# Heads 12 and 13 of a dilated attention layer: queries and keys moved through DRAM instead of transposed on TensorE

## The chip, the cores and the metric

One core of one Trainium2 chip runs the whole kernel. The metric is the device time of one execution in microseconds (us). Beside it stands a profile of one execution, whose span runs from its first to its last instruction. In the text TensorE (PE in the profile) multiplies matrices, VectorE is DVE, ScalarE is ACT, GpSimd is POOL, and SyncE (SP) issues nearly all DMAs; its queue runs in order.

## The reference

An encoder block of two layers on 512 tokens of width 1024, 16 heads of 64. Only the first layer is touched here. In it every head has three dilation groups (dilations 1, 4, 16), each with its own queries, keys and values, and the three results are merged by their softmax denominators:

```python
def mixer_a(hn, w_in, w_out, q_gain, k_gain, t5_bias):
    proj = hn @ w_in
    qkv = proj[..., :n_qkv].reshape(b, s, N_DIL_GROUPS, 3, N_HEADS, HEAD_DIM)
    gate = proj[..., n_qkv:]
    for g, (window, dilation) in enumerate(DILATED_PAIRS):      # (128, 1), (512, 4), (2048, 16)
        q = rms_norm(qkv[:, :, g, 0], q_gain[g])
        k = rms_norm(qkv[:, :, g, 1], k_gain[g])
        v = qkv[:, :, g, 2]
        o, lse = dilated_group_attention(q, k, v, t5_bias[...], dilation, reach)
        ...
    alpha = jax.nn.softmax(jnp.stack(lses), axis=0)
    y = jnp.sum(alpha[..., None] * jnp.stack(outs), axis=0)
    y = y.reshape(b, s, BRANCH_WIDTH) * jax.nn.silu(gate)
    return y @ w_out
```

The second layer (neighbourhood attention) follows on the sum of input and output, with the same kind of projections, gate and output product.

## The kernel before

Heads go in pairs: hc = 0 to 7 counts pairs, NHC = 8, and heads 12 and 13 are hc = 6. For each pair main_a issues four projections, each a run of matmuls with 512 columns: the keys of groups 1 and 2 with their values (rawk, 96 matmuls), the queries of all three groups with the keys of group 0 (rawq, 96), the values of group 0 (v0_a, 24) and the gate (gate_a, 24). Products are taken in three matmuls each (high and low parts of both operands), so three matmuls are the smallest group. For hc = 7 rawq stands ahead of rawk, and gate 6 comes after both: rawq(7), rawk(7), gate(6), v0(7), gate(7). Then follows the output projection, out_product.

A projection is gathered in four PSUM banks (ps_acc), one for each quarter of the tokens; a bank is free again when ScalarE has evicted it (line 551). After the last quarter the rows are normalised for each head (head_norm): squares on GpSimd (line 317), a sum on VectorE, the factor rs by rsqrt on VectorE or GpSimd, and a scaling on VectorE (line 337).

Scores want queries and keys with the head dimension on the partitions. There are two ways to it.

- For hc = 0 to 5 (moved(hc)): VectorE turns blocks of 32 by 32 in place (turn_raw, line 588), move_q writes the tile rq of queries and keys to a DRAM tile qd (1.5 MB), and four reads bring it back into qt in the other order (lines 722 and 729). Then split_q on ScalarE scales and copies into k0 and three areas of queries (lines 793 and 777).
- For hc = 6 and 7: k_a and q_a transpose on TensorE, four blocks of 128 by 128 at a time (transpose4), two times for k_a and four for q_a, and evict each four with one instruction into qt and k0 (lines 679, 705, 712, 793).

The values of group 0 already take a similar way through DRAM (move_v) for hc = 0 to 6.

attn_a computes the scores of a pair in two halves, u = 0 and u = 1, 96 matmuls in the profile each ("log"). Each half goes through softmax on VectorE and ScalarE (p), is turned on VectorE into tr, written to DRAM (td) and read back into pt (class turner). When both halves are back, weigh() multiplies with the values ("o") and put_y applies the gate. weigh of pair hc is run inside the first half of pair hc + 1 ("pending").

The order on TensorE is the order of the program. Two generators make it: main yields after each group of three projection matmuls, and run() lets side insert its pieces when they are due. Due times are counted on a clock that adds an estimate for each matmul:

```python
        cols = max(r.free_size() / 2.4, l.free_size() / 1.2)
        clock[0] += (cols if r.dtype == F32R else r.free_size() * 4 / 2.4 * l.free_size() / P) / share
```

`yield "wait", (key, hc), 6500` makes the side wait until the stamp (key, hc) is set and the clock has gone 6500 beyond it; `later_on(delay, job)` puts a job, mostly a DMA, into the program at clock + delay. A guard, such as ("q", hc - 1) in main_a, keeps the last step of a projection from being issued before the stamp is set. The tiles rq (raw queries and keys), qt, k0, tr and pq are single buffers. The other engines' orders come from the scheduler, apart from instructions pinned by keep_in_program_order. Weights are loaded by SyncE in pieces of 512 KB (wraw, three buffers), split by splits() into high and low parts (wh and wl, four buffers each) on ScalarE, VectorE and GpSimd, at least three pieces ahead of use.

Of the kernel before, what the change touches and what calls it, by code (L numbers as in the profile page):

```python
# [26 lines left out]
NHC = 8  # L27
# [25 lines left out]
def tile_hybrid_encoder(  # L53
# [168 lines left out]
                yield h[:, c : c + n], l[:, c : c + n]  # L222

    clock = [0.0]
    stamp = {(key, -1): 0 for key in ("k12", "q", "v", "qk")}
    stamp |= {(key, -i, "y"): 0 for key in ("ya", "yb") for i in range(1, 6)}

    def matmul(o, l, r, share=1, **kw):
# [283 lines left out]
        fs, f0, f1 = FS[key]  # L512
        return rq[:, : 512 * fs].rearrange("p (a x) -> p a x", a=4)[:, :, P * f0 : P * f1]

    moved = lambda hc: hc < NHC - 2

    def part(n):
        return rk[:, 1024 * n : 1024 * n + 1024].rearrange("p (i c) -> p i c", i=4)
# [57 lines left out]
        normed(raw, ss, ns, key, hc)  # L576

    def normed(raw, ss, ns, key, hc):
        delay = (11000 if moved(hc) else 9000) if key == "rawk" and 0 < hc < NHC - 1 else 0
        head_norm(raw, ss, ns, delay, then=partial(turn_raw, key) if moved(hc) else None)  # L580
        st[key, hc] = raw
        stamp[key, hc] = clock[0]

# [49 lines left out]
    def move_v(hc, vt):  # L633

        d = dr.tile([4, P, P], F32, name="vd", tag="vd", bufs=2)
        vx = vv[:, S:].rearrange("p (b i r) -> p b i r", b=4, i=4)
        nc.vector.transpose(vx.rearrange("p b i r -> p i b r"), vt.rearrange("p (i b r) -> p i b r", i=4, b=4))

        def write():
            tc.keep_in_program_order(nc.sync.dma_start(d.rearrange("b p x -> p b x"), vx.rearrange("p b i r -> p b (i r)")))  # L640

        def read(b):
            dst = vt[32 * b : 32 * b + 32].rearrange("k (a x) -> k a x", a=4)
            tc.keep_in_program_order(nc.sync.dma_start(dst, d[b].rearrange("(a k) x -> k a x", a=4)))

        def place():
            src = vt.rearrange("p (a i r) -> p i a r", a=4, i=4)
            dst = v0[hc % 2].rearrange("p i (a r) -> p i a r", a=4)
            tc.keep_in_program_order(nc.scalar.copy(dst, src))
            stamp["v", hc] = 0  # L650

        out, back, there = (8000, 15000, 23500) if moved(hc) else (8000, 13000, 18500)
        later_on(out, write)
        for b in (0, 2, 1, 3):
            later_on(back, partial(read, b))
        later_on(there, place)

    def main_a(hc):
        parts = (
            project_qk(512, 4, "rawk", hc, ("k12" if hc == NHC - 1 else "q", hc - 1), first=hc == 0, need=None if hc else "na"),  # L660
            project_qk(512, 8, "rawq", hc, ("q", hc - 1) if hc else ("rs", "a")),
        )
        yield from chain(*(parts[::-1] if hc == NHC - 1 else parts))
        if hc == NHC - 1:
            yield from gate_a(hc - 1)
        yield from v0_a(hc)
        if hc != NHC - 2:
            yield from gate_a(hc)

    def k_a(hc):  # L670
        if moved(hc):
            return
        yield "wait", ("rawk", hc), 35000 if hc < NHC - 1 else 10500
        qt = q_tiles(hc)[0]
        raw = st.pop(("rawk", hc))
        for g in range(2):
            tp = transpose4(raw, g * P)
            dst = qt[:, :, 4 + g, :].rearrange("p t (j r) -> p t j r", j=4)
            nc.vector.tensor_scalar(dst, to_tjr(tp), gk[:, g + 1 : g + 2], None, op0=ALU.mult)
            yield  # L680
        stamp["k12", hc] = 0

    def q_tiles(hc):

# [7 lines left out]

    def q_a(hc):

        yield "wait", ("rawq", hc), 8000 if moved(hc) else 18500 if hc < NHC - 1 else 23500
        raw = st.pop(("rawq", hc))
        if moved(hc):
            move_q(hc)
            return
        qt, k0 = q_tiles(hc)  # L700

        by_t = lambda to: qt[:, :, to, :].rearrange("p t (x r) -> p x t r", x=16)
        of_t = lambda tp: tp.rearrange("p (x t r) -> p x t r", x=16, t=4)
        tp = transpose4(raw, 0)
        nc.scalar.copy(by_t(0), of_t(tp))
        yield
        tp = transpose4(raw, 3 * P)
        scaled(trj(k0[:, 64:EXT]), to_trj(tp), 0)
        yield
        for g in range(2):  # L710
            tp = transpose4(raw, (g + 1) * P)
            nc.vector.tensor_copy(by_t(1 + g), of_t(tp))
            yield
        stamp["q", hc] = 0

    def move_q(hc):

        d = dr.tile([4, P, 768], F32, name="qd", tag="qd", bufs=2)
        left = [4]

        def write():
            tc.keep_in_program_order(nc.sync.dma_start(d.rearrange("a p x -> p a x"), rq.rearrange("p (a x) -> p a x", a=4)))
            stamp["q", hc] = 0

        def read(a):
            qt, _ = q_tiles(hc)
            dst = qt[32 * a : 32 * a + 32].rearrange("k t f x -> k t (f x)")
            src = d[a].rearrange("(t k) x -> k t x", t=4)
            tc.keep_in_program_order(nc.sync.dma_start(dst, src))
            left[0] -= 1  # L730

        later_on(600, write)

        def land():
            for a in (0, 2, 1, 3):
                later_on(6500, partial(read, a))
            yield "wait", ("rawk", hc + 1), 0
            assert not left[0]
            split_q(hc, *q_tiles(hc))
            yield  # L740

        st["land", hc] = land
# [35 lines left out]

    def v_a(hc):

        if hc < NHC - 1:
            return
        yield "wait", ("vt", hc), 2500
        vt = st.pop(("vt", hc))
        tp = bank("tp")
        for i in range(4):
            transpose(tp[:, i * P : (i + 1) * P], vt[:, i * P : (i + 1) * P])
        nc.scalar.copy(v0[hc % 2], tp.rearrange("p (i c) -> p i c", i=4))
        stamp["v", hc] = 0
        yield  # L790
# [148 lines left out]
    def attn_a(hc):  # L939
# [114 lines left out]

        if hc < NHC - 1:
            for u in range(2):
                if moved(hc):
                    if u == 0:
                        yield "wait", ("rawk", hc + 1), 6500
                    elif hc < NHC - 3:  # L1060
                        yield "wait", ("open", hc + 1), 2500
                    else:
                        yield "wait", ("rawq", hc + 1), 2500
                else:
                    yield 6500 if u == 0 else 7000
                turned = turner(512)
                turners.append(turned)
                for hd, t, pr in scores(u):
                    turned.put(pr, 512, 256 * hd + 64 * (t % 2), 128)
                send = partial(turned.send, pq[:, 2048 * u : 2048 * u + 2048], *((6000, 500) if u else (8500, 1200)))  # L1070
                later_on(7000 + 2000 * u, send)
                if pending and u == 0:
                    yield 7500 if moved(hc) else 5000
                    pending.pop(0)()
                    yield 0
                if moved(hc) and u == 0:
                    yield "half"
            pending.append(lambda: put_y(hc, weigh(), True, False))
        else:
            for u in range(2):  # L1080
                if u == 0:
                    yield "wait", ("gate", hc), 500
                yield 600
                held = scores(u)
                yield 3200
                if pending:
                    yield "wait", ("gate", hc - 1), 16800
                    pending.pop(0)()
                    yield
                for args in held:  # L1090
                    turn_p(*args)
                    yield
            yield from v_a(hc)
            stamp["ya", "turned"] = 0
            put_y(hc, weigh(), True, True)
            yield
# [260 lines left out]
    def side():  # L1357
# [21 lines left out]
        halves = []  # L1379
        for hc in range(NHC):  # L1380
            if hc < NHC - 1:
                if not moved(hc):
                    yield from halves.pop(0)
                yield from k_a(hc)
                yield from chain(q_a(hc), v_a(hc))
                if moved(hc):
                    if hc:
                        yield from halves.pop(0)
                    yield from st.pop(("land", hc))()
                half = attn_a(hc)  # L1390
                for v in half:
                    if v == "half":
                        if hc == 2:
                            bias_rows()
                        halves.append(half)
                        break
                    yield v
            else:
                gap[0] = cycle((500, 500, 700))
                yield from chain(q_a(hc), k_a(hc))  # L1400
                yield from attn_a(hc)
        yield from residual(xg, 0)
# [129 lines left out]
```

## Time and profile before

| | us |
|---|---|
| median of 3 runs | 812.57 |
| lowest and highest run | 811.8 and 812.92 |
| profiled execution, device time | 813.07 |
| profiled execution, span | 811.3 |
| busy in the span: PE, DVE, ACT, POOL | 805.1, 537.9, 445.4, 233.9 |
| granted TensorE clock, mean | 1.000 |

The profile's page gives busy time by engine, the chain of work that ended last, and groups of instructions by line. A timeline row holds the start, the length, the engine, the line, the operation, output <- inputs, and in brackets the idle time before it with what ended it. Matmuls overlap in their records (0.39 us long, a new one each 0.23 us), so distances between starts tell the time that TensorE takes. "tp" is a bank with transposes, "acc" a bank of a projection. Loads to PE's weight side are PEld; SPq is SyncE's DMA queue, and a DMA's row there is its issue, not its transfer.

### The profile page before, as it was taken

The page shows a single profiled execution, that of the slowest core. Times are in us where ns is not written, and L with a number is a line of the kernel's source. Part 1 is how long each engine was busy: PE and PEld are TensorE (multiplying, and loading weights), DVE is VectorE, ACT ScalarE, POOL GpSimd, SP SyncE. Part 2 cuts the span into 40 slices and gives each one's busy share as a digit, 9 for nine tenths or more (in the row PEclk, how much of TensorE's full clock was granted, in tenths as well). Part 3 has the DMA queues.
Part 4 walks back from the last instruction along what each step waited for, and adds up shares of the span by engine and source line. Part 5 has one row for each costly group of instructions (what it writes and reads, how often), then busy time and mean ns, then how long its engine had stood idle before and what let it go on. Part 6 is the DMA issues. An engine that isn't in the chain of part 4 may idle for free.

```text
span 811.3 us, 16466 instructions
## 1 busy us (share of the span) xinstructions
PE 805.1 (99%) x6100; PEld 658.7 (81%) x6100; DVE 537.9 (66%) x1364; ACT 445.4 (55%) x931; POOL 233.9 (29%) x388
## 2 busy tenths in 40 slices
PE   9999999999999999999999999999999999999998
PEld 7888888888888888888888877888888887778787
DVE  7366475676567487577467775639646989897824
ACT  7352745745745655744745564536336675757720
POOL 2251532431441431532532342211222315040100
PEclk9999999999999999999999999999999999999999
DMA  7378777976976996976985565167354887688664
GB/s 263 93 199 272 211 206 216 264 208 190 276 219 198 284 261 219 292 228 209 288 234 165 157 208 139 49 202 248 106 183 123 235 244 213 201 266 239 181 209 157
DMA packets 92481, 169.43 MB, mean 209 GB/s; under 512 B 12080, under 2 KB 51136, under 8 KB 92400
## 3 DMA queue, kind: packets, MB, share of 16 engines
q1 hardware_dynamic: 92256, 168.11, 70.6%
q8 instruction: 48, 0.79, 0.4%
q14 instruction: 33, 0.27, 0.1%
q10 hardware_dynamic: 144, 0.26, 0.1%
HBM read 126.26 MB, written 48.24 MB: 215 GB/s over the span
## 4 chain that ended last, share of the span: by engine, by line
PE 91%; DVE 4%; ACT 3%; DMA 1%; issue 1%; POOL 0%; SPq 0%; DVEq 0%; ACTq 0%
PE acc L232 81%; PE log L232 5%; PE o L232 4%; PE tp L236 1%; DVE wl L139 1%; ACT p L1290 1%; ACT p L1296 1%; DMA t<-in_t5x 0%; DMA x<-in_xt 0%; ACT rawq L551 0%; DVE rawq L337 0%; ACT wh L133 0%; ACT p L1010 0%; DVE na L120 0%; PE pa L232 0%
## 5 line engine op out<-in xcount | busy, mean ns | idle before, releaser
L232 PE MATMUL acc<-wh,hn_h 128*128 128x512 f32 x704 | 279.0, 397 | 1.1 <-ACT hn_h L429 0.8
L232 PE MATMUL acc<-wl,hn_h 128*128 128x512 f32 x704 | 274.5, 391 | 0.0
L232 PE MATMUL acc<-wh,hn_l 128*128 128x512 f32 x704 | 274.2, 390 | 0.0
L133 ACT CAST wh<-wraw 128x512 fp32r<-128x512 f32 (+1 forms) x240 | 145.8, 613 | 191.0 <-PE acc L232 162.5
L139 DVE TENSOR_TENSOR wl<-wraw,wh 128x512 fp32r<-128x512 f32 (+1 forms) x169 | 126.0, 747 | 139.4 <-ACT wh L133 139.0
L139 POOL TENSOR_TENSOR wl<-wraw,wh 128x512 fp32r<-128x512 f32 (+1 forms) x72 | 95.4, 1326 | 222.2 <-ACT wh L133 177.2
L232 PEld LDWEIGHTS acc<-wh,hn_h 128*128 128x128 f32 x704 | 132.5, 188 | 32.6 <-issue 3.1
L232 PEld LDWEIGHTS acc<-wh,hn_l 128*128 128x128 f32 x704 | 132.7, 188 | 28.2
L232 PEld LDWEIGHTS acc<-wl,hn_h 128*128 128x128 f32 x704 | 132.8, 189 | 26.7 <-POOL wl L139 0.3
L317 POOL TENSOR_TENSOR sq<-rawq 128x256 f32<-128x256 f32 (+1 forms) x84 | 61.2, 738 | 109.5 <-ACT rawq L551 91.1
L232 PE MATMUL acc<-y,wh 128*128 128x512 f32 (+1 forms) x272 | 81.5, 383 | 0.0
L232 PE MATMUL acc<-hn_h,wh 128*128 128x512 f32 x192 | 75.6, 394 | 0.5 <-ACT rawk L551 0.5
L1010 ACT ACTIVATE p<-p,mn 128x512 f32<-128x512 f32 (+1 forms) x64 | 44.8, 701 | 56.8 <-DVE mn L999 56.7
L232 PE MATMUL acc<-hn_l,wh 128*128 128x512 f32 x192 | 74.7, 389 | 0.0
L232 PE MATMUL acc<-hn_h,wl 128*128 128x512 f32 x192 | 74.7, 389 | 0.0
L918 DVE STREAM_TRANSPOSE tr<-p 128x512 f32<-128x512 f32 (+1 forms) x88 | 59.3, 681 | 19.9 <-ACT p L837 10.5
L318 DVE TENSOR_REDUCE ss<-sq 128x4 f32<-128x256 f32 (+1 forms) x96 | 47.7, 505 | 32.5 <-POOL sq L317 32.1
L232 PEld LDWEIGHTS acc<-y,wh 128*128 128x128 f32 x272 | 48.8, 188 | 9.4 <-issue 0.9
L337 DVE TENSOR_TENSOR rawq<-rawq,rs 128x256 f32<-128x256 f32 (+1 forms) x96 | 49.6, 577 | 5.3 <-POOL rs L125 5.0
L232 PE MATMUL acc<-y,wl 128*128 128x512 f32 (+1 forms) x136 | 51.3, 377 | 0.0
L551 ACT ACTIVATE rawq<-acc,rs_n 128x512 f32<-128x512 f32 (+1 forms) x76 | 45.8, 613 | 0.3
L837 ACT ACTIVATE p<-p,mn 128x512 f32<-128x512 f32 (+1 forms) x64 | 44.6, 701 | 0.2 <-DVE mn L836 0.2
(147 smaller groups left out, 946.5 us busy)
## 6 DMA issues: line engine op xcount, KB each, us to landing
wraw<-in_w SPq DMA_DIRECT2D x111, 512.0 KB, 4.8
td<-tr SPq DMA_DIRECT2D x14, 1024.0 KB, 8.1
pt<-td SPq DMA_DIRECT2D x56, 256.0 KB, 5.7
qd<-rawq SPq DMA_DIRECT2D x6, 1536.0 KB, 7.6
qt<-qd SPq DMA_DIRECT2D x24, 384.0 KB, 6.3
td<-tr SPq DMA_DIRECT2D x8, 896.0 KB, 4.9
pt<-td SPq DMA_DIRECT2D x32, 224.0 KB, 6.7
v0x<-in_w SPq DMA_DIRECT2D x8, 512.0 KB, 5.9
```

Source lines behind the costliest of these rows:

```text
L133: nc.scalar.copy(h, raw)
L139: eng.tensor_sub(l, raw, h.bitcast(F32))
L232: nc.tensor.matmul(o, l, r, **kw)
L236: nc.tensor.transpose(o, i, ident)
L317: nc.gpsimd.tensor_mul(to, v, v)
L318: nc.vector.tensor_reduce(ss[:, i * ns : (i + 1) * ns], sq.rearrange("p (a b) -> p a b", b=64), axis=AX.X, op=ALU.add)
L337: m = nc.vector.tensor_mul(v, v, by)
L551: nc.scalar.activation(dst, src, AF.Copy, scale=rs_n[:, i : i + 1])
L837: nc.scalar.activation(pr, pr, AF.Copy, scale=mn[:, 3:4])
L918: nc.vector.transpose(dst, src[:, :n].rearrange(order, b=4, k=32, **({"g": 2} if apart else {})))
L1010: nc.scalar.activation(row, row, AF.Exp, bias=mn[:, 1:2], scale=-1.0, accum_out=mn[:, 2:3])
L1290: nc.scalar.activation(pr[:, o : o + n], pr[:, o : o + n], AF.Exp, bias=mn[:, 0:1], scale=-1.0, accum_out=mn[:, 2:3])
```

## The change

moved(hc) now holds for hc = 6 too. So that pair's queries and keys are turned on VectorE, written to DRAM and read back, and k_a and q_a transpose on TensorE for hc = 7 alone. With it, delays change: the second scores of hc = 5 wait for 9000 after rawq(6) instead of 2500; the reads of hc = 6 are put 5000 after them; the scores of hc = 6 wait for rawq(7) + 6500 and rawq(7) + 23200; hc = 7's transposes wait longer (rawq + 30500 and rawk + 12000); the weighing of hc = 6 waits for its gate + 18500; and the factors of the normalisation of rawk(7) are made on VectorE (quick). The guard on rawk(7) is now ("q", 6), as for the other pairs.

```diff
-    moved = lambda hc: hc < NHC - 2
+    moved = lambda hc: hc < NHC - 1
...
-        delay = (11000 if moved(hc) else 9000) if key == "rawk" and 0 < hc < NHC - 1 else 0
-        head_norm(raw, ss, ns, delay, then=partial(turn_raw, key) if moved(hc) else None)
+        delay = 11000 if key == "rawk" and 0 < hc < NHC - 1 else 0
+        head_norm(raw, ss, ns, delay, key == "rawk" and hc == NHC - 1, then=partial(turn_raw, key) if moved(hc) else None)
...
-        out, back, there = (8000, 15000, 23500) if moved(hc) else (8000, 13000, 18500)
-        later_on(out, write)
+        later_on(8000, write)
         for b in (0, 2, 1, 3):
-            later_on(back, partial(read, b))
-        later_on(there, place)
+            later_on(15000, partial(read, b))
+        later_on(23500, place)
...
-            project_qk(512, 4, "rawk", hc, ("k12" if hc == NHC - 1 else "q", hc - 1), first=hc == 0, need=None if hc else "na"),
+            project_qk(512, 4, "rawk", hc, ("q", hc - 1), first=hc == 0, need=None if hc else "na"),
...
     def k_a(hc):
-        if moved(hc):
-            return
-        yield "wait", ("rawk", hc), 35000 if hc < NHC - 1 else 10500
+        yield "wait", ("rawk", hc), 12000
...
-        yield "wait", ("rawq", hc), 8000 if moved(hc) else 18500 if hc < NHC - 1 else 23500
+        yield "wait", ("rawq", hc), 8000 if moved(hc) else 30500
...
             for a in (0, 2, 1, 3):
-                later_on(6500, partial(read, a))
-            yield "wait", ("rawk", hc + 1), 0
+                later_on(6500 if hc < NHC - 2 else 5000, partial(read, a))
+            yield "wait", ("rawk" if hc < NHC - 2 else "rawq", hc + 1), 0
...
-                if moved(hc):
-                    if u == 0:
-                        yield "wait", ("rawk", hc + 1), 6500
-                    elif hc < NHC - 3:
-                        yield "wait", ("open", hc + 1), 2500
-                    else:
-                        yield "wait", ("rawq", hc + 1), 2500
+                if u == 0:
+                    yield "wait", ("rawk" if hc < NHC - 2 else "rawq", hc + 1), 6500
+                elif hc < NHC - 3:
+                    yield "wait", ("open", hc + 1), 2500
+                elif hc == NHC - 3:
+                    yield "wait", ("rawq", hc + 1), 9000
                 else:
-                    yield 6500 if u == 0 else 7000
+                    yield "wait", ("rawq", hc + 1), 23200
...
-                    yield "wait", ("gate", hc - 1), 16800
+                    yield "wait", ("gate", hc - 1), 18500
...
             if hc < NHC - 1:
-                if not moved(hc):
+                yield from q_a(hc)
+                if hc:
                     yield from halves.pop(0)
-                yield from k_a(hc)
-                yield from chain(q_a(hc), v_a(hc))
-                if moved(hc):
-                    if hc:
-                        yield from halves.pop(0)
-                    yield from st.pop(("land", hc))()
+                yield from st.pop(("land", hc))()
...
             else:
                 gap[0] = cycle((500, 500, 700))
+                yield from halves.pop(0)
                 yield from chain(q_a(hc), k_a(hc))
```

More of the change, by code (lines that the diff above doesn't have):

```diff
@@ L224, in tile_hybrid_encoder @@
     clock = [0.0]
-    stamp = {(key, -1): 0 for key in ("k12", "q", "v", "qk")}
+    stamp = {(key, -1): 0 for key in ("q", "v", "qk")}
     stamp |= {(key, -i, "y"): 0 for key in ("ya", "yb") for i in range(1, 6)}
@@ L680, in k_a @@
             yield
-        stamp["k12", hc] = 0
     def q_tiles(hc):
@@ L779, in v_a @@
     def v_a(hc):
-        if hc < NHC - 1:
-            return
         yield "wait", ("vt", hc), 2500
@@ L1072, in attn_a @@
                 if pending and u == 0:
-                    yield 7500 if moved(hc) else 5000
+                    yield 7500
                     pending.pop(0)()
                     yield 0
-                if moved(hc) and u == 0:
+                if u == 0:
                     yield "half"
```

## The prediction

> **What bounds the kernel now.** I read the page's engine shares first, then the chain of waits, then the timelines of TensorE, VectorE and the SyncE queue around heads 12 and 13.
>
> ```profile
> PE 805.1 (99%) x6100; PEld 658.7 (81%) x6100; DVE 537.9 (66%) x1364; ACT 445.4 (55%) x931; POOL 233.9 (29%) x388
> ```
>
> This is busy time by engine. TensorE is busy 805.1 of 811.3 us, so the order of its instructions is the time: what leaves it shortens the run, unless its place is taken by a wait. The other engines have slack and matter only where TensorE ends up waiting for them. The chain of waits shows what one matmul and one block of four transposes cost (start, length, what, count):
>
> ```profile
> 42.83 51.03 PE acc L232 x225
> ...
> 440.44 0.44 PE tp L236 x4
> 440.88 1.39 PE acc L232 x6
> 442.27 0.44 PE tp L236 x4
> ...
> 453.42 1.84 PE log L232 x96
> ...
> 460.94 2.72 PE o L232 x120
> ```
>
> 225 matmuls in 51.03 us are 0.2268 us each. Six matmuls with four transposes take 442.27 - 440.44 = 1.83 us; six alone would take 1.36. So four transposes cost 0.47 us in place. A set of scores (log) takes 1.84, a weighing (o) 2.72, and some 0.1 each at its borders.
>
> **The change, part by part.** (1) *Transposes.* For hc = 6 k_a runs two blocks of four and q_a four: 24 transposes leave TensorE. 6 x 0.47 = 2.82 us. From below: the transposes alone, 6 x 0.44 = 2.64; nothing hides them, as the matmuls on both sides run without a gap.
>
> The Trainium skill ("TensorE: Matmul & The Clock Gate", Part 4) gives some 275 ns for a 128x128 transpose inside a kernel; by that, as an estimate, 24 would be worth 6.6 us. The rows above disagree with it as a price of TensorE time: 0.47/4 = 0.12 us.
>
> (2) *The bank wait at the end of hc = 7's keys.* TensorE's timeline before:
>
> ```profile
> 478.04 0.39 PE L232 MATMUL acc<-wh,hn_l 128*128 128x512 f32 x1
> 478.27 0.60 PE L236 MATMUL tp<-ident,rawq 128*128 128x128 f32 x4
> 478.62 0.48 PE L232 MATMUL acc<-wh,hn_h 128*128 128x512 f32 x1
> ...
> 479.87 0.39 PE L232 MATMUL acc<-wh,hn_l 128*128 128x512 f32 x1
> 480.10 0.60 PE L236 MATMUL tp<-ident,rawq 128*128 128x128 f32 x4
> 481.23 0.50 PE L232 MATMUL acc<-hn_h,wh 128*128 128x512 f32 x1 [0.53 <-ACT rawk L551]
> ```
> ```profile
> 479.74 0.72 ACT L837 ACTIVATE p<-p,mn 128x512 f32<-128x512 f32 x1
> 480.36 0.46 ACT L551 ACTIVATE rawq<-acc,rs_n 128x256 f32<-128x256 f32 x1
> ```
>
> Around an ordinary block the matmuls stand 0.58 us apart (478.04 to 478.62); here 1.36 (479.87 to 481.23): 0.78 us lost. The gate's first matmul needs the bank of the keys' first quarter, and ScalarE evicts that only after the eight softmax passes of the scores at 471.30, the last at 479.74. After the change these scores stand six matmuls before the keys' end. I count in the planner's clock by the formula in matmul(): 640 a group of three, 1600 a set of scores, 2453 a weighing. From the end of rawq(7): 11 groups reach 6500 and scores(6,0) goes in; 12 more reach its 7500, weigh(5); 7 more reach 23200 (18,773 + 7 x 640 = 23,253), scores(6,1); 30 of 32 groups are done. So the evictions of quarters 0 and 1 are issued ahead of the softmax, and the gate finds its bank free after about 2 + 1.4 us. Quarters 2 and 3 are evicted late, but their banks are wanted only by the gate 10.9 us on and by the output projection. Saved: 0.78; if ScalarE runs the softmax first after all, 0.
>
> (3) *hc = 7's keys.* Before, the first transposes of k_a(7) trickled behind the normalisation, whose factors GpSimd made:
>
> ```profile
> 492.95 1.33 PE L236 MATMUL tp<-ident,rawq 128*128 128x128 f32 x4
> 494.03 0.48 PE L232 MATMUL acc<-hn_h,wh 128*128 128x512 f32 x1
> ```
> ```profile
> 485.90 0.53 POOL L113 TENSOR_SCALAR nv<-ss 128x16 f32<-128x16 f32 x1
> ...
> 492.21 0.22 POOL L125 TENSOR_TENSOR rs<-rs,na 128x16 f32<-128x16 f32 x1
> ```
>
> 494.03 - 492.95 = 1.08 instead of 0.35: 0.73 us lost. Now VectorE makes the factors (quick), and the delay is 12000 instead of 10500. GpSimd's chain took 492.43 - 485.90 = 6.5 us; no row quoted here prices the same chain on VectorE, and the last two evictions still come after the softmax. If the factors are there in time the whole 0.73 is saved, if not, nothing; the two steps of delay point the same way, so I take a little over half: -0.4 (0 to -0.73).
>
> (4) *Queries and keys through DRAM: when are they back?* Added: on VectorE two transposes of keys and two of queries (0.69 and 1.22 us each), on ScalarE split_q and two squares, on SyncE one write of 1.5 MB and four reads; removed: four evictions on VectorE, two on ScalarE, two squares on GpSimd. These engines are 66, 55 and 29% busy, so the work costs nothing by itself; its lateness may. The pattern before is that of hc = 5 (rawq ends at 356.24, where v's first matmul starts) and, for the reads, hc = 4; the last row is both transfers' landing.
>
> ```profile
> 356.24 0.39 PE L232 MATMUL acc<-hn_h,wh 128*128 128x512 f32 x1
> ...
> 369.93 0.66 PE L232 MATMUL log<-k,q 64*32 64x256 f32 x16
> ...
> 417.74 0.39 PE L232 MATMUL acc<-hn_h,wh 128*128 128x512 f32 x1
> ...
> 420.55 0.66 PE L232 MATMUL log<-k,q 64*32 64x256 f32 x16
> ```
> ```profile
> 366.50 2.50 DVE L337 TENSOR_TENSOR rawq<-rawq,rs 128x512 f32<-128x512 f32 x4
> ...
> 369.52 2.37 DVE L588 STREAM_TRANSPOSE rawq<-rawq 128x1024 f32<-128x1024 f32 x2
> ```
> ```profile
> 260.98 2.21 SPq L729 DMA_DIRECT2D qt<-qd  x4
> ...
> 371.92 0.38 SPq L722 DMA_DIRECT2D qd<-rawq  x1
> ```
> ```profile
> 270.92 1.24 ACT L793 ACTIVATE k<-qt,gk 128x512 f32<-128x512 f32 x1 [1.26 <-DMA qt<-qd]
> ...
> 272.57 1.33 ACT L793 ACTIVATE q<-qt,gk 128x512 f32<-128x512 f32 x2
> ```
> ```profile
> qd<-rawq SPq DMA_DIRECT2D x6, 1536.0 KB, 7.6
> qt<-qd SPq DMA_DIRECT2D x24, 384.0 KB, 6.3
> ```
> ```profile
> DMA to landing us min/median/max: 4.4/7.0/8.6
> ```
>
> rawq(5) ends at 356.24, its write leaves at 371.92, 15.7 us on, when VectorE is done; it lands in 7.6. hc = 4's reads start at 260.98 and the last is in at 270.92, where ScalarE had waited for it: 9.9 us. The split then takes until 273.90, 3.0 us. Now hc = 6: rawq(6) ends at 417.74, so write 433.4, landed 441.0, reads back 450.9, split done 453.9. TensorE: from 417.74, 45 matmuls (15 groups, past 9000) to scores(5,1) at 427.9; 1.94 us for these; 75 more end rawq(7) at 446.9; 33 more: scores(6,0) at 454.4. The margin is 0.5 us, and a cast or two of 0.6 us may stand inside the split. While the split waits at the head of ScalarE's queue, from about 448 on, the casts of weights stand behind it; splits() keeps three pieces ahead, 36 matmuls or 8.2 us, against 5.9 us until 453.9. I take 0.3 us of wait, 0 to 2.0 (landing in 8.6 instead of 7.6, and both casts inside). What it covers else: the eviction of rawq(7) into the same tile starts at about 445, 4 us after the write has landed.
>
> The Trainium skill ("DMA: Bandwidth & Descriptors", Anatomy of one DMA) speaks against such moves: a DMA's semaphore waits for the last byte's receipt, slowest into HBM. Its fit, made for GpSimd's path, is 2.0 us plus bytes/436 GB/s, as an estimate 5.6 us a hop; by that the split would be done by 448 with no wait and the sum 0.3 better. The rows' 7.6 and 9.9 decide.
>
> (5) *The SyncE queue.* The four reads stand in program order 5000 after scores(5,1), about 435; the queue waits there up to 6 us for the write, and behind it are weight loads, v's reads and td(5,1). Weights have cover:
>
> ```profile
> 473.15 0.38 SPq L197 DMA_DIRECT2D wraw<-in_w  x1
> ...
> 481.48 0.38 SPq L927 DMA_DIRECT2D td<-tr  x1
> 485.85 4.48 SPq L197 DMA_DIRECT2D wraw<-in_w  x2
> 490.43 1.80 SPq L931 DMA_DIRECT2D pt<-td  x4
> ```
>
> 12.7 us between two loads, and no matmul waited. td(5,1) leaves about 443, is back by 460, and weigh(5) stands at 464.6: nothing. weigh(6) has less room than before: scores(6,1) at 472.2, td 10.2 us on (as 471.30 to 481.48), reads 9.0 later, back within 9: 500.4. weigh(6) stood at 506.97 and comes forward with everything else to 503.3. Cover 2.9 us instead of some 7; cost 0.
>
> ```profile
> 471.30 0.45 PE L232 MATMUL log<-k,qt 64*32 64x256 f32 x8
> ```
> ```profile
> 506.97 0.34 PE L232 MATMUL o<-pt,rawk 64*64 64x128 f32 x4
> ```
>
> **Sum.** -2.82 - 0.78 - 0.4 + 0.3 = -3.7 us. The profiled execution took 813.07 us (span 811.3, 1.8 around it), so its counterpart is 809.4; it lies 0.5 above the median of the runs, 812.57, and against that the forecast is 808.9 (-0.46%). Own range: all gains without wait, 812.57 - 4.33 = 808.2; no gain in (3) and 2.0 us of wait, 812.57 - 3.6 + 2.0 = 811.0.
>
> **Rivals.** *A: VectorE takes the softmax of scores(5,1) ahead of the queries' normalisation; slower.* That is the order before in hc = 6:
>
> ```profile
> 433.62 4.08 DVE L337 TENSOR_TENSOR rawq<-rawq,rs 128x512 f32<-128x512 f32 x4
> ```
>
> There scores(5,1) came 2.8 us after rawq(6) (420.55) and the scaling began 15.9 after it, not 10.3 as in hc = 5. With both transposes the write would leave at 440.1, land at 447.7 (rawq(7)'s eviction waits too), be back at 457.6, split 460.6: scores(6,0) wait 6.2 us. 812.57 - 4.0 + 6.2 = 814.8. It turns slower than before once the wait passes 4.0 us, a write after about 437.9. For it: the scores now come 10.2 us after rawq(6), in hc = 5 13.7 (369.93 after 356.24), and scaling starts at +10.3; against: the scaling is then ready first and was issued first. 0.14.
>
> *B: the same path 2 to 4 us late, or weigh(6) past its cover by as much.* The gain is eaten: 812.57 - 4.0 + 3 = 811.6 to 812.6. 0.13.
>
> *C: the transposes are worth their full length, 24 x 0.277 = 6.6 us:* 812.57 - 6.6 - 0.9 = 805.1.
>
> ```profile
> L236 PE MATMUL tp<-ident,rawq 128*128 128x128 f32 x48 | 7.9, 277 | 0.0
> ```
>
> The start times speak against it. The skill's figure would be this case. 0.02.
>
> **How the numbers follow.** 0.71 for the forecast, 0.14 A, 0.13 B, 0.02 C. A measurement here tells about 0.2%, 1.6 us. Faster: forecast nearly whole, C: 0.73. Within 0.2%: B: 0.13. Slower: A: 0.14. The range 808.0 to 812.4 leaves out A, C and the tail of B.
>
> **What would show it.** Right: 24 fewer transposes; no idle before the first gate matmul behind rawk(7); scores(6,0) directly behind a matmul, about 454; k_a(7)'s block in 0.6 us; everything from the output projection on shifted by one amount. Wrong: a write of qd later than 437.9, TensorE idle before the scores of hc = 6 with ScalarE's split as the releaser, or before weigh(6) with a DMA.

## The result, and the profile after

| | before | after |
|---|---|---|
| median of the runs, us | 812.75 (811.8 to 813.26, 4 runs) | 807.65 (806.89 to 809.32, 4 runs) |
| profiled execution, us | 813.07 | 808.28 |
| its span, us | 811.3 | 806.4 |

The ratio of the times is 0.9939, with an interval from 0.9927 to 0.9951: the changed kernel is 0.6% faster. The median is 1.25 us below the forecast of 808.9 and 0.35 below the low end of the range.

The first part of the page, busy time by engine, after:

```profile
PE 799.7 (99%) x6076; PEld 654.5 (81%) x6076; DVE 539.4 (67%) x1375; ACT 447.6 (56%) x935; POOL 229.5 (28%) x372
```

24 matmul instructions fewer, and TensorE is busy 5.4 us less. It still fills 99% of the span, so its timeline tells where the time went. TensorE's timeline after, at the places that the prediction named:

```profile
417.46 0.39 PE L232 MATMUL acc<-hn_h,wh 128*128 128x512 f32 x1
...
454.31 0.56 PE L232 MATMUL log<-k,q 64*32 64x192 f32 x16
...
475.59 0.39 PE L232 MATMUL acc<-hn_h,wh 128*128 128x512 f32 x1
...
489.01 0.60 PE L236 MATMUL tp<-ident,rawq 128*128 128x128 f32 x4
...
494.70 0.61 PE L232 MATMUL acc<-y,wh 128*128 128x512 f32 x2
...
502.30 1.57 PE L232 MATMUL o<-pt,rawk 64*64 64x128 f32 x64
```

Read downwards, no row has idle time in brackets: neither the scores of hc = 6 (454.31) nor the gate's first matmul behind rawk(7) (475.59) nor weigh(6) (502.30) waits, and the first block of k_a(7) (489.01) takes 0.60 us. Two marks serve in all that follows: v's first matmul of hc = 6, and the first matmul of the output projection. Between them lies nearly everything that the change touches. Before, the second mark is this row:

```profile
499.36 0.62 PE L232 MATMUL acc<-y,wh 128*128 128x512 f32 x2
```

Before, the stretch took 499.36 - 417.74 = 81.62 us; after, 494.70 - 417.46 = 77.24: 4.38 us gone. The other 0.5 of the 4.9 us between the spans lie outside: 0.28 ahead of the first mark, the rest behind the second.

### The profile page after: what moved, and what is told of

It reads as the page before. It is cut to its first block, busy times and chain, and to the rows that moved or that the text cites. A ratio compares the mean times of both kernels' runs of the same rounds, so it can differ in the third digit from the quotient of the medians.

```text
span 806.4 us, 16425 instructions
## 1 busy us (share of the span) xinstructions
PE 799.7 (99%) x6076; PEld 654.5 (81%) x6076; DVE 539.4 (67%) x1375; ACT 447.6 (56%) x935; POOL 229.5 (28%) x372
## 4 chain that ended last, share of the span: by engine, by line
PE 62%; DVE 3%; ACT 2%; issue 0%; POOL 0%; DVEq 0%
PE acc L232 55%; PE log L232 3%; PE o L232 3%; ACT p L1283 1%; PE tp L236 1%; DVE wl L139 1%; ACT p L1289 1%; DVE rawq L337 0%; ACT rawq L551 0%; DVE rawq L744 0%; POOL sq L317 0%; DVE ss L318 0%; DVE gt L865 0%; DVE qkb L1239 0%; DVE qkb L1235 0%
## 5 line engine op out<-in xcount | busy, mean ns | idle before, releaser
L139 DVE TENSOR_TENSOR wl<-wraw,wh 128x512 fp32r<-128x512 f32 (+1 forms) x169 | 123.9, 735 | 134.6 <-ACT wh L133 134.3
```

The costliest lines, as they stand in the source:

```text
L139: eng.tensor_sub(l, raw, h.bitcast(F32))
```

## Experiments

**The kernel before, profiled once more.** No edit.

> The kernel before, unaltered, profiled once more. It tells how far the same instructions scatter from execution to execution. Theory: the stretch from v's first matmul of hc = 6 to the output projection's first repeats within 0.1 us of 81.62, the gate's first matmul waits 0.5 us behind rawk(7) again and k_a(7)'s block takes 1.2 to 1.4 us; the point at which v's first matmul of hc = 6 stands lies between 416.3 and 418.0 and carries nearly all of the difference in device time between this execution and the earlier one (813.07). Rival (the stretch itself scatters by as much as the terms of the sum): 80.9 to 82.3, and waits of other sizes.

Its timeline on TensorE:

```profile
416.43 0.39 PE L232 MATMUL acc<-hn_h,wh 128*128 128x512 f32 x1
...
479.94 0.50 PE L232 MATMUL acc<-hn_h,wh 128*128 128x512 f32 x1 [0.54 <-ACT rawk L551]
...
498.03 0.62 PE L232 MATMUL acc<-y,wh 128*128 128x512 f32 x2
```

498.03 - 416.43 = 81.60: the stretch repeats within 0.02 us, and so do its waits (0.54 here; k_a(7)'s first block takes 1.33 again). The first mark does not: 416.43 instead of 417.74, and this execution took 811.81 instead of 813.07 us. So the scatter arises ahead of the mark. Terms of tenths of a microsecond can be read from the stretch, but not from device times, which scatter by more than 1 us.

**The changed kernel, profiled once more.** No edit.

> The changed kernel once more, unaltered. Theory: the change takes 4.3 us of TensorE time (2.8 transposes, 0.8 wait for a bank, 0.7 wait for the last keys) and the rest of the difference of the medians, 5.1 us, is the scatter of single executions: the distance from the first values matmul after rawq(6) to the end of the last matmul should repeat within 0.1 us, while the time from the start of the span to that matmul may differ by 1 us or more. Over more rounds the ratio to the kernel before should then come nearer to 0.9947 (4.3 of 812.6) than to 0.9939. Rival: the excess over 4.3 us is real and outside the region around heads 12 and 13; then the ratio stays at 0.9939 or below and the distance from the start repeats at 417.5 us.

807.17 us median (806.93 to 808.59, 5 runs), ratio 0.9941 [0.993, 0.9953]. The stretch runs from 416.40 to 493.67, 77.27 us. The pair of second profiles, 811.81 and 807.17 us, differs by 4.64: 81.60 - 77.27 = 4.33 in the stretch, some 0.03 ahead of it, and 0.24 to 0.28 behind it. That last piece stands in all pairs: from the second mark to the span's end it is 311.9 to 312.0 us in the three profiles with all transposes and 311.7 to 311.85 in the changed kernel and its variants (the last experiment apart, where other work stands around the mark). It is not TensorE's: the last matmul starts 308.38 to 308.44 us after the second mark in before, the changed kernel, the second profiles of both and the kernel with the changed times alone. So the piece lies behind the last matmul, around the eviction and the DMA of the last output; what makes it is not known. Of the expectation, the stretch and the moving first mark came true (416.40 instead of 417.46); the ratio did not move towards 0.9947, but both 0.9939 and 0.9947 lie inside its interval.

**The changed times alone, transposes kept.** Before's kernel with the second scores of hc = 6 put six matmuls ahead of the end of rawk(7), hc = 7's delays of the change, and quick:

```diff
-        head_norm(raw, ss, ns, delay, then=partial(turn_raw, key) if moved(hc) else None)
+        head_norm(raw, ss, ns, delay, key == "rawk" and hc == NHC - 1, then=partial(turn_raw, key) if moved(hc) else None)
...
-        yield "wait", ("rawk", hc), 35000 if hc < NHC - 1 else 10500
+        yield "wait", ("rawk", hc), 35000 if hc < NHC - 1 else 12000
...
-        yield "wait", ("rawq", hc), 8000 if moved(hc) else 18500 if hc < NHC - 1 else 23500
+        yield "wait", ("rawq", hc), 8000 if moved(hc) else 18500 if hc < NHC - 1 else 30500
...
-                    yield 6500 if u == 0 else 7000
+                    yield 6500 if u == 0 else 10800
...
-                    yield "wait", ("gate", hc - 1), 16800
+                    yield "wait", ("gate", hc - 1), 18500
```

> The kernel before, in which heads 12 and 13 keep their transposes on TensorE, but with the changed times: the second scores of hc = 6 six matmuls ahead of the end of rawk(7), hc = 7's transposes after rawq + 30500 and rawk + 12000, and the factors of rawk(7) on VectorE. Theory: the two waits go (0.8 and 0.7 us), the transposes' 2.8 us stay; from the first values matmul after rawq(6) to the first matmul of the output projection it takes 1.5 us less than before (81.6 to 80.1), and the time is 0.2% below the kernel before. Rival: the transposes cost next to nothing in place and the gain of the change comes from its times; then this kernel takes nearly the whole 4.3 us off.

811.93 us median (810.42 to 812.56, 11 runs), ratio 0.9988 [0.9976, 1.0]. TensorE's timeline:

```profile
417.64 0.39 PE L232 MATMUL acc<-hn_h,wh 128*128 128x512 f32 x1
...
478.61 0.39 PE L232 MATMUL acc<-hn_h,wh 128*128 128x512 f32 x1
...
492.06 1.18 PE L236 MATMUL tp<-ident,rawq 128*128 128x128 f32 x4
492.99 0.48 PE L232 MATMUL acc<-hn_h,wh 128*128 128x512 f32 x1
...
498.31 0.61 PE L232 MATMUL acc<-y,wh 128*128 128x512 f32 x2
```

The stretch is 80.67 us, 0.95 shorter than before. The gate's first matmul, at 478.61, has no wait any more; the transposes of k_a(7) still trickle, 492.99 - 492.06 = 0.93 instead of 0.35, 0.58 lost. What sets this kernel apart from the changed one is the 24 transposes and that wait: 80.67 - 77.27 = 3.40, less 0.58, leaves 2.82 for the transposes, the prediction's 6 x 0.47.

**Second scores 18 matmuls ahead instead of six.**

```diff
-                    yield "wait", ("rawq", hc + 1), 23200
+                    yield "wait", ("rawq", hc + 1), 20600
```

> The changed kernel, but the second scores of hc = 6 stand 18 matmuls ahead of the end of rawk(7) instead of six (their wait is 20600 after rawq(7) instead of 23200). Theory (the bank wait depends on whether ScalarE's eviction of the keys' first quarter is queued ahead of these scores' softmax or behind it): the scores come about 2.7 us earlier, ScalarE takes the softmax passes ahead of the eviction, and the gate's first matmul waits again, 0.8 to 2.3 us with the eviction of rawk(7)'s first quarter as the releaser; the keys' factors may be late for k_a(7) as well, another 0 to 0.6. From v's first matmul of hc = 6 to the output projection's first 78 to 79.5 us, against 77.25 in the changed kernel. Rival (the bank is free because the scores stand between the projection's end and the gate no more, wherever ahead they are): no wait, 77.25. Device time 808 to 810 by the theory, 807.4 by the rival.

One execution took 810.21 us, a little above the 808 to 810 expected; the stretch runs from 417.48 to 496.71, 79.23 us, 1.96 longer than in the changed kernel's second profile. The gate's first matmul on TensorE, and ScalarE's work around it:

```profile
477.43 0.50 PE L232 MATMUL acc<-hn_h,wh 128*128 128x512 f32 x1 [1.40 <-ACT rawk L551]
```
```profile
471.95 0.72 ACT L1004 ACTIVATE p<-p,mn 128x512 f32<-128x512 f32 x1 [1.37 <-DVE mn L993]
...
476.47 0.19 ACT L1004 ACTIVATION_READ_ACCUMULATOR p<-p,mn 128x1 f32 x1
476.57 0.45 ACT L551 ACTIVATE rawq<-acc,rs_n 128x256 f32<-128x256 f32 x1
```

Here the eviction of the first quarter (line 551) comes behind the softmax passes of the early scores, which begin at 471.95. In the changed kernel ScalarE had taken it ahead of them:

```profile
471.68 0.47 ACT L551 ACTIVATE rawq<-acc,rs_n 128x256 f32<-128x256 f32 x1
...
475.40 0.73 ACT L1004 ACTIVATE p<-p,mn 128x512 f32<-128x512 f32 x1 [2.14 <-DVE mn L993]
```

The theory holds: it is the order on ScalarE that decides, and scores that come 12 matmuls too early cost more (1.96) than scores behind the projection's end (0.78).

**Factors of rawk(7) on GpSimd, as before.**

```diff
-        head_norm(raw, ss, ns, delay, key == "rawk" and hc == NHC - 1, then=partial(turn_raw, key) if moved(hc) else None)
+        head_norm(raw, ss, ns, delay, False, then=partial(turn_raw, key) if moved(hc) else None)
```

> The changed kernel, but the factors of the normalisation of rawk(7) are made on GpSimd as before the change (quick off). Theory (k_a(7)'s transposes come without a wait because the evictions of rawk(7) start earlier, not because VectorE makes the factors faster: 6.4 us there, 6.5 on GpSimd): the factors are ready at about the same time, the block of k_a(7) takes 0.6 to 0.75 us and stands 0.35 to 0.5 from the next matmul; from v's first matmul of hc = 6 to the output projection's first 77.25 to 77.4 us. Rival (VectorE's chain is what saved the 0.7 us): the transposes trickle again, the block takes 1.2 to 1.3 us, and the distance is 77.9 to 78.0. Device time 807.4 by the theory, 808.1 by the rival.

The theory falls. One execution took 808.80 us (807.4 by the theory, 808.1 by the rival). The stretch runs from 417.10 to 495.05, 77.95 us, 0.7 longer, and the block trickles again. TensorE's block, VectorE's last sum and scaling, and the start of GpSimd's chain in this kernel:

```profile
488.71 1.25 PE L236 MATMUL tp<-ident,rawq 128*128 128x128 f32 x4
```
```profile
480.36 0.42 DVE L318 TENSOR_REDUCE ss<-sq 128x4 f32<-128x256 f32 x1 [0.40 <-POOL sq L317]
...
488.14 1.43 DVE L337 TENSOR_TENSOR rawq<-rawq,rs 128x256 f32<-128x256 f32 x4 [2.44 <-POOL rs L125]
```
```profile
480.52 1.29 POOL L139 TENSOR_TENSOR wl<-wraw,wh 128x512 fp32r<-128x512 f32 x1
481.90 0.20 POOL L113 TENSOR_SCALAR nv<-ss 128x16 f32<-128x16 f32 x1
...
485.44 1.29 POOL L139 TENSOR_TENSOR wl<-wraw,wh 128x512 fp32r<-128x512 f32 x1
```

And VectorE in the changed kernel:

```profile
480.73 0.42 DVE L318 TENSOR_REDUCE ss<-sq 128x4 f32<-128x256 f32 x1 [0.41 <-POOL sq L317]
481.18 1.02 DVE L113 TENSOR_SCALAR nv<-ss 128x16 f32<-128x16 f32 x1
...
487.63 1.43 DVE L337 TENSOR_TENSOR rawq<-rawq,rs 128x256 f32<-128x256 f32 x4
```

From its first operation to the scaling the chain is no shorter on VectorE: 481.18 to 487.6 is 6.4 us, 481.90 to 488.1 on GpSimd 6.2. Both times hold other work too, on GpSimd a second split of weights (485.44, 1.29). But GpSimd begins 1.54 us after the start of the last sum (480.36 to 481.90), because a split of weights (480.52, 1.29) has just started there; VectorE begins 0.45 after it. From the last sum to the scaling it is 7.78 us against 6.90. With the scaling's 1.43 the changed kernel's keys are ready at 489.06, when the block's place is 489.01: nothing is to spare, and 0.9 us later costs 0.7.

Is VectorE's chain enough? VectorE before, and ScalarE's eviction of the third quarter in the kernel with the changed times alone:

```profile
484.30 0.42 DVE L318 TENSOR_REDUCE ss<-sq 128x4 f32<-128x256 f32 x1 [0.31 <-POOL sq L317]
...
492.46 1.43 DVE L337 TENSOR_TENSOR rawq<-rawq,rs 128x256 f32<-128x256 f32 x4 [1.59 <-POOL rs L125]
```
```profile
481.56 0.45 ACT L551 ACTIVATE rawq<-acc,rs_n 128x256 f32<-128x256 f32 x1
```

The four kernels side by side, in us after the end of rawk(7) on TensorE (480.10 before, the start of the gate's first matmul in the others):

| | before | changed times alone | factors on GpSimd | changed |
|---|---|---|---|---|
| last sum starts | 4.20 | 6.24 | 5.13 | 5.14 |
| scaling is done | 13.79 | 14.24 | 14.34 | 13.47 |
| first block of k_a(7) starts | 12.85 | 13.45 | 13.48 | 13.42 |
| scaling is done after that start by | 0.94 | 0.79 | 0.86 | 0.05 |
| lost at the block | 0.73 | 0.58 | 0.65 | 0 |

The kernel with the changed times alone had VectorE's chain and lost 0.58 all the same: there ScalarE evicted the third quarter 2.95 us after the gate's start (478.61 to 481.56) instead of 1.85, two softmax passes later, and the last sum came 1.1 us later. So both are needed: VectorE's chain, and evictions that come as early as in the changed kernel. Against before, the changed kernel's last sum is not earlier but 0.94 us later. Two things make up for this and for the 0.94 by which the keys were late: VectorE, with 6.90 from the last sum to the scaling instead of 8.16, and the block's place, 0.57 us later (the delay of 12000 for 10500). The later place was not tried alone.

**First scores of hc = 6 earlier.**

```diff
-                    yield "wait", ("rawk" if hc < NHC - 2 else "rawq", hc + 1), 6500
+                    yield "wait", ("rawk" if hc < NHC - 2 else "rawq", hc + 1), 6500 if hc < NHC - 2 else 2500
```

> The changed kernel, but the first scores of hc = 6 wait for 2500 after rawq(7) instead of 6500, so they stand some 20 matmuls, about 4.8 us, earlier: 449.5 instead of 454.3 in the profiled changed kernel. It measures the cover of the transfer through DRAM. Theory (split done about 1.9 us ahead of the scores in the changed kernel, and its time set by the write, the reads and the split alone): TensorE waits 2 to 4 us (middle 3) before these scores, the split on ScalarE as the releaser; weigh(5), which comes forward with them, may wait for its reads by up to 1 us. From v's first matmul of hc = 6 to the output projection's first 80 to 81.5 us against 77.25. Rival (queries and keys are back much earlier than the profile's rows say, or the scheduler orders ScalarE by TensorE's need and so brings the split forward): wait under 1 us, at most 78.2. Device time 810 to 811.5 by the theory, under 808.5 by the rival.

TensorE and ScalarE where the scores are:

```profile
449.25 0.56 PE L232 MATMUL log<-k,q 64*32 64x192 f32 x16 [0.89 <-ACT q L773]
449.87 1.07 PE L232 MATMUL log<-qt,q 64*32 64x128 f32 x32
```
```profile
447.45 1.24 ACT L787 ACTIVATE k<-qt,gk 128x512 f32<-128x512 f32 x1 [0.57 <-DMA qt<-qd]
```

Between theory and rival: one execution took 808.80 us, and the stretch is 416.20 to 495.32, 79.12 us, 1.85 longer than 77.27, where 2.75 to 4.25 were expected. The scores don't wait for the whole split. The first 16 start when its second instruction is done (line 773; 0.89 us idle), the next 32 run beside the third, stretched to 1.07 us. And the reads were back 0.7 us earlier: the split starts 447.45 - 416.20 = 31.25 us after the first mark, against 31.95 in the changed kernel (449.41 - 417.46). The scores stand 21 matmuls, 4.8 us, earlier and lose some 1.65 there (0.96 ahead of them, 0.69 within); so the cover of the whole transfer in the changed kernel is 4.8 - 1.65 - 0.7, about 2.4 us.

**Softmax of scores(5,1) ahead of the queries' normalisation.** The second scores of hc = 5 right behind rawq(6), as before, and ahead of move_q in the side's order; this makes rival A:

```diff
-                    yield "wait", ("rawq", hc + 1), 9000
+                    yield "wait", ("rawq", hc + 1), 2500
...
+                if hc == NHC - 2:
+                    yield from halves.pop(0)
                 yield from q_a(hc)
-                if hc:
+                if 0 < hc < NHC - 2:
                     yield from halves.pop(0)
```

> The changed kernel, in which the second scores of hc = 5 stand 2500 after rawq(6) again, ahead of the write's place, so that VectorE meets their softmax before the normalised queries are turned. Theory (the mechanism of the prediction's rival A): the write of the queries leaves 5 to 8 us later than the changed kernel's 431.7, their way back pushes the split past the place of the first scores of hc = 6, and TensorE waits there 3 to 6 us; the gain of the change is gone. Rival: the margin is larger than thought or the write is not held back, TensorE waits less than 1 us, and the time is that of the changed kernel.

813.88 us median (812.72 to 815.52, 10 runs), ratio 1.0021 [1.0012, 1.003]: slower than before, and the stretch, 417.18 to 499.93, is 82.75 us, 5.5 longer than in the changed kernel. SyncE's queue, ScalarE, TensorE:

```profile
434.22 0.38 SPq L718 DMA_DIRECT2D qd<-rawq  x1
434.81 0.38 SPq L921 DMA_DIRECT2D td<-tr  x1
...
439.77 4.53 SPq L725 DMA_DIRECT2D qt<-qd  x4
444.35 5.00 SPq L925 DMA_DIRECT2D pt<-td  x4
```
```profile
456.10 1.17 ACT L787 ACTIVATE k<-qt,gk 128x512 f32<-128x512 f32 x1 [6.63 <-DMA qt<-qd]
```
```profile
457.83 0.89 PE L232 MATMUL log<-k,q 64*32 64x192 f32 x16 [2.79 <-ACT q L773]
```

The write leaves 17.0 us after the first mark, 2.8 later than in the changed kernel (431.68 - 417.46 = 14.2), where 5 to 8 were expected. The reads take 16.3 us from their first issue to the last landing (439.77 to 456.10), against 12.1 in the changed kernel. The write of td, 1 MB, overlaps them in both. New beside them are the four reads of pt, from 444.35 on, which in the changed kernel leave only after qt is back; I take them for the cause, though no run separates it. TensorE waits 2.79 us, 0.68 more for a bank behind rawq(7)'s late eviction, and then runs the scores slowly: 461.34 - 457.83 = 3.5 us instead of 1.84. Busy time by engine in one microsecond of it (the granted clock is the third last column, ahead of the DMA share and GB/s):

```profile
458.00:459.00 1.00, 1.00 (x32) 0.39 (x25) 0.00 (x0) 1.00 (x3) 0.00 (x0) 0.50 1.05 258
```

**One step further.** The changed kernel, with the first half of hc = 7's softmax sent through VectorE and DRAM as well instead of four blocks of transposes on TensorE:

```diff
-                    yield "wait", ("gate", hc), 500
-                yield 600
+                    yield "wait", ("gate", hc), 0
+                yield 0 if u == 0 else 4600
                 held = scores(u)
+                if u == 0:
+                    turned = turner(512)
+                    turners.append(turned)
+                    for hd, t, pr in held:
+                        turned.put(pr, 512, 256 * hd + 64 * (t % 2), 128)
+                    held = []
+                    later_on(7000, partial(turned.send, pq[:, :2048], 5500, 200))
...
+            yield 4500
             yield from v_a(hc)
```

Its first scores are put at the end of gate(7), and weigh(7) keeps its place behind the last piece.

> The changed kernel, with the first half of the softmax of hc = 7 turned on VectorE and sent through DRAM as for the other pairs, instead of four blocks of four transposes on TensorE with their four evictions; its first scores stand at the end of gate(7), and the weighing of hc = 7 at the last place that the output projection allows. Theory: each block leaves 0.47 us, so 1.9 us less than the changed kernel, if the half is back by the weighing at about 522.8 us; from the rows of hc = 6's second half (27 us from scores to landing) it is back at about 522, so a wait of up to 1 us may stand there and the gain lies between 0.9 and 1.9. Rival: with all 16 transfers and the weights in one queue the half comes back later than 524.7 and the gain is lost.

805.75 us median (805.35 to 807.49, 6 runs), ratio to before 0.9925 [0.9913, 0.9937]. 16 transposes fewer. weigh(7) on TensorE:

```profile
522.11 1.57 PE L232 MATMUL o<-pt,rawk 64*64 64x128 f32 x64
```

It starts without a wait, 105.76 us after the first mark, against 107.62 (524.02) in the changed kernel's second profile: 1.86 us, four blocks of 0.47. The median is 1.4 us below the changed kernel's 807.17; the intervals of the two ratios still overlap, so the 1.86 rests on the profiles.

## Why the prediction was right or wrong

**(1) Transposes: right.** 2.82 us predicted, 2.82 measured between the kernel with the changed times alone and the changed kernel. In place a block of four costs 0.47 us, and four further blocks were worth the same. Rival C, with 6.6 us, is refuted. The 275 ns that the Trainium skill ("TensorE: Matmul & The Clock Gate", Part 4) gives for one agree with the length recorded here (277 ns on average) and not with this price, 0.12 us each.

**(2) Bank wait: right.** 0.78 predicted; it went where the second scores stand six matmuls ahead, with and without transposes, and came back as 1.40 us of idle time where they stand 18 ahead.

**(3) Keys of hc = 7: the direction right, the size wrong.** I took -0.4, a little over half of the bound, because no row priced the chain on VectorE. The whole 0.73 went (block of 0.60 instead of 1.33). The two parts together just sufficed, with 0.05 us between the block's place and the keys: 1.26 us by VectorE and 0.57 by the later place, against evictions that put the last sum 0.94 later. Of the 1.26, 1.15 lie ahead of the chain's first operation and not in the chain: before, GpSimd began it 1.60 us after the start of the last sum (484.30 to 485.90), behind a split of weights (484.53, 1.29) that the timeline of before would have shown. Nor did the last two evictions come behind the whole softmax: ScalarE took the third quarter's between two passes.

```profile
477.44 0.45 ACT L551 ACTIVATE rawq<-acc,rs_n 128x256 f32<-128x256 f32 x1
```

**(4) Queries and keys back through DRAM: mis-sized by the full +0.3.** There is no wait. SyncE, VectorE and ScalarE after:

```profile
431.68 0.38 SPq L718 DMA_DIRECT2D qd<-rawq  x1
...
437.20 1.75 SPq L725 DMA_DIRECT2D qt<-qd  x4
...
445.04 0.38 SPq L921 DMA_DIRECT2D td<-tr  x1
...
454.07 1.75 SPq L925 DMA_DIRECT2D pt<-td  x4
```
```profile
426.75 2.50 DVE L337 TENSOR_TENSOR rawq<-rawq,rs 128x512 f32<-128x512 f32 x4
```
```profile
449.41 1.25 ACT L787 ACTIVATE k<-qt,gk 128x512 f32<-128x512 f32 x1 [1.28 <-DMA qt<-qd]
...
451.07 1.33 ACT L787 ACTIVATE q<-qt,gk 128x512 f32<-128x512 f32 x2
```

Against the predicted 433.4, 441.0, 450.9 and 453.9 stand 431.7 (write), 437.1 (landed; the reads leave then), 449.3 (back) and 452.4 (split done), all to be read with the 0.28 us by which this execution was ahead. VectorE scaled 9.3 us after the first mark, not 10.3, and turned at once; the write took 5.4 us, not 7.6; the reads 12.1, not 9.9; the split 3.0, as predicted, with no cast inside. Two errors of 2.2 us cancelled, and the earlier VectorE was left. The Trainium skill's fit ("DMA: Bandwidth & Descriptors", Anatomy of one DMA), made for GpSimd's path, by which a hop of 1.5 MB takes an estimated 5.6 us, agrees with the write's 5.4 and gives less than half of the 12.1 that the four reads took.

**(5) Covers: right.** Neither weigh(5) nor weigh(6) waits, and no matmul waited for weights there.

**Sum.** With (3) whole and (4) at nothing it is -4.33; the stretch shows -4.38 and, in the second pair, -4.33. That is the case that the prediction called all gains without wait, 808.2. The medians lie 0.5 to 1 us lower: 0.25 of it is the unexplained piece behind the last matmul; the rest is within the scatter of the medians themselves (before 812.57, 812.75 and 812.5; after 807.65 and 807.17). So two steps failed: the sizes of (3), -0.4 for a measured -0.73, and of (4), +0.3 for a measured 0, 0.63 us together; and the low end of the range was too tight, as it allowed 0.2 us beyond the best case where executions of one kernel scatter by more than 1 us.

**Rival A** starts from the right step and has nearly the right price (1.4 us slower than before by the medians, 2.2 forecast), but by another way: the write left at 434.2, well ahead of the 437.9 from which I held that it decides. By the prediction's own durations the split would have been done at 434.2 + 7.6 + 9.9 + 3.0 = 454.7, and the scores, due at about 454.0 in that execution, would hardly have waited. Of the 7.0 us by which the split began later than in the changed kernel, only 2.8 are the late write's; 4.1 are the reads', which took 16.3 us. What I had left out is that scores(5,1) also bring the reads of pt into the same stretch, the likely cause, and that the clock falls behind such a wait. **Rival B** did not come; about 2.4 us of cover kept it away.

## What to carry to other kernels

Where TensorE fills the span, price a removed block by the distance of its neighbours' starts, not by its recorded length, and read the change from a stretch between two marks, since device times of one kernel scatter by more than such terms. Before halving an unknown, look at what stands in the queue ahead of it: a wait that a change of engine removes may be the other engine's queue and not its speed. And a step that is brought forward brings its own transfers with it: count everything that shares a stretch with a transfer that TensorE waits for (here only argued, from the reads that took 16.3 us instead of 12.1).

## What was not expected of the hardware

In the kernel with the softmax of scores(5,1) first, TensorE was idle for 2.8 us (455.0 to 457.8) and then ran at a granted clock of 0.50 until about 461.2, some 3.4 us; the scores there took 3.5 us instead of 1.84. So this wait cost another 1.7 us, most of it by the clock: the second 32 matmuls may also have waited for the split's third part, beside which they ran. Of this kernel's ten executions eight have a mean clock of 0.997 or 0.998; the two with 1.000 took 812.72 and 812.86 us and are the fastest. So the clock is not halved in every execution; how long TensorE waited in those two is not on record. After 0.9 us of idle time ahead of the same scores, and 1.4 ahead of the gate, no such loss shows. The Trainium skill ("TensorE: Matmul & The Clock Gate", Part 1) gives half the clock after an idle window of about 3.4 us, until a window of about that length has been busy; the trace agrees with the length of the slow part, and 2.8 us of idle time were enough in this profile.

The four reads of 384 KB took 9.9 us for hc = 4 before, 12.1 for hc = 6 in the changed kernel and 16.3 where the reads of pt went beside them. In the changed kernel, busy time in the middle of the reads:

```profile
440.00:445.00 5.00, 5.00 (x24) 4.14 (x23) 1.27 (x4) 1.57 (x4) 1.30 (x1) 1.00 1.01 215
```

The DMA engines were wholly busy (1.01) and moved 215 GB/s; which transfer slowed which was not tried.
